# A two-layer mLSTM and RG-LRU trunk on one core: pair 7 of the FFN's input product in seven products, and half of its output weights' low halves by accumulating DMAs

## The chip, the core and the metric

The kernel runs on one core of a Trainium2 chip. A core has five engines with instruction queues of their own: TensorE (PE, with its weight loads as PEld) multiplies, VectorE (DVE) and ScalarE (ACT) work element by element, GpSimd (POOL) does a few small things and can issue DMAs, SyncE (SP) issues most DMAs. Each engine takes its instructions in the order in which they stand in its queue and waits on semaphores for the others. The metric is the time of one execution on the device, in microseconds (us); less is better.

## What is computed

One sequence of 256 tokens with 2048 features goes through two layers. Layer 0 has a chunkwise mLSTM mixer, layer 1 an RG-LRU mixer; each is followed by a SwiGLU feed-forward network (FFN), all in float32:

```python
D_MODEL, SEQ, D_FF = 2048, 256, 5632

def swiglu(x, w_in, w_out):
    g, u = jnp.split(x @ w_in, 2, axis=-1)
    return (jax.nn.silu(g) * u) @ w_out

for layer in range(2):
    h = h + mixer(rms_norm(h, norm_mix[layer]), ...)
    h = h + swiglu(rms_norm(h, norm_ffn[layer]), ffn_w_in[layer], ffn_w_out[layer])
return rms_norm(h, norm_final)
```

The change lies in the FFN, which runs once in each layer.

## The kernel before

**Three matmuls for one product.** TensorE takes operands rounded to a shorter float32 form (`F32R`). Every operand is therefore split into a rounded high half and the rest as a low half (`split`: ACT rounds, DVE subtracts), and a product takes three matmuls: high by high, high by low, low by high (`product`, lines 819 to 821). Of each weight tile, 512 KB or 1 MB in float32, ACT makes `whi` and DVE makes `wlo`.

**The FFN's loop.** `ffn` walks over j = 0 to 10, each a block of 512 of the 5632 inner columns; one pass is called a turn here. In a turn `inner` multiplies the 256 tokens by the gate and the up block of the first weights. The 2048 input features are taken as eight pairs p = 0 to 7 of row tiles of 128. A pair is a two by two block product: two row tiles of the features by two token halves, against gate (B11, B21) and up (B12, B22) blocks. A *plain* pair takes eight products (24 matmuls of 512 columns); a pair in `SEVENS` takes seven (21 matmuls) by Strassen's scheme in Winograd's form: DVE first makes four sums T1 to T4 of the weight blocks (`sum`, lines 312, 315, 316), so there are seven weight tiles to split, three of raw blocks (`whix`, `wlox`, 128x1536) and four of sums (`whit`, `wlot`, two instructions of 128x1024 each). The features' side of the seven (`SEVEN`) is prepared once per layer by `NormPairs.pair`.

**The banks.** Seven PSUM banks hold the sums: Q5, P2, Q3 and P4, which a plain pair writes too, and P1, Q6 and P7, which only pairs in seven products write. Pair 7 is plain and is the last, so P1, Q6 and P7 are complete after pair 6; then ACT copies P1 to `ds` (line 853) and DVE forms d0 and d1 from Q6 and P7 (lines 854, 856). After pair 7 DVE adds Q5, P2, Q3 and P4 (lines 859 to 865), ACT applies silu, DVE multiplies (line 868): these are the 512 inner activations of 256 tokens in `ds`. In the next turn PE transposes them (`tv`), and ACT and DVE split them into `hh`. In turn 0 pairs 1 to 4 (`BOTH`) are plain too.

**The second layer of the FFN.** For each turn's `hh`, `outs` makes eight pieces: a quarter q of the 2048 output columns by a token half b, 12 matmuls each (`out`). They are put between the products of the next turn, one per pair, from pair 4 of one turn to pair 3 of the one after. Ahead of b = 0, the quarter's weights come in two loads of 512 KB by SP (`rawo`, i = 0 and 1), and each is split into `whio` and `wloo`. These tiles have one buffer for each i. The last pieces of a layer use other tiles.

**What sets the order.** The code is recorded with priorities, and a scheduler with its own estimates sets the order in each engine's queue; splits and combinations have a raised priority. `whi` and `wlo` of the first weights have three buffers each, in rotation over all weight tiles of the pairs; the raw tiles too.

Of the kernel before, what the change touches and what calls it, by code (L numbers as in the profile page):

```python
# [42 lines left out]
def kernel(  # L43
# [117 lines left out]
    mask = const.tile([P, P], F32, name="mask")  # L161
    nc.gpsimd.memset(mask, 0.0)
    nc.gpsimd.affine_select(
        out=mask, in_=mask, compare_op=ALU.is_ge, fill=BIG, base=0,
        pattern=[[1, P]], channel_multiplier=-1,
    )
# [631 lines left out]
    def ffn(layer, n, nxt):  # L798
# [86 lines left out]
        def outs(j, hi, lo):  # L885
# [7 lines left out]
            def load(q, last):  # L893
# [9 lines left out]
                for i in range(2):  # L903
                    raw, wh, wl = (
                        pool_of(f"{what}o").tile([P, 2, NB], dt, tag=f"{what}{i}", name=f"{what}o{j}{q}{i}")
                        for what, dt in (("raw", F32), ("whi", F32R), ("wlo", F32R))
                    )
                    nc.sync.dma_start(raw, wv[:, 2 * i:2 * i + 2, q * NB:(q + 1) * NB])
# [300 lines left out]
```

## Time and profile before

| | |
|---|---|
| Median of 3 runs | 2086.08 us (2085.92 to 2087.57) |
| The profiled execution | 2085.02 us, of which the instructions' span is 2083.2 us |
| PE busy | 2069.3 us, 99% of the span |
| DVE busy | 1742.1 us, 84% |
| ACT busy | 1343.0 us, 64% |
| POOL busy | 43.2 us, 2% |
| Granted TensorE clock, mean | 0.999 |
| HBM read | 401.84 MB, 194 GB/s over the span |
| The FFN of layer 0, of layer 1 | from about 398 us, and from about 1383 us |

An engine's busy time says how much of the span it had something to do, not that it set the pace. A wait counts where an engine that sets the pace stands still. Rows of groups give the line of the code, the engine, the operation, out<-in by tile names, and behind the bar the busy time, the mean duration in ns, and idle time with its releaser.

### The profile page before, as it was taken

To read this page: it belongs to the slowest core of one execution; us is meant where nothing else is said; L and a number is where in the kernel's file an instruction comes from. 1 tells how busy PE (TensorE), PEld (TensorE's weight loads), DVE (VectorE), ACT (ScalarE), POOL (GpSimd) and SP (SyncE) were. 2 spreads that over 40 slices of the span, in tenths; PEclk is the share of its full clock that TensorE was granted. 3 is DMA by queue.
4 is the path that set the end of the run, shared out by engine and by line. 5 is a ranking of instruction groups with operands and counts; after the bars stand their busy time and mean duration, and the time that the engine had idled before them with its cause. 6 is when DMAs were issued, how large, how long until landed. Compare 5 with 4: busy or idle time off the path is not lost.

```text
span 2083.2 us, 27536 instructions
## 1 busy us (share of the span) xinstructions
PE 2069.3 (99%) x10484; PEld 1752.6 (84%) x10484; DVE 1742.1 (84%) x1898; ACT 1343.0 (64%) x1627; POOL 43.2 (2%) x62
## 2 busy tenths in 40 slices
PE   9999999999999999999999999999999999999998
PEld 8988888887888888888889999888788888888886
DVE  6655556699999999999976787679999999999995
ACT  6344446566777676777764768556676776776774
POOL 0011110000000000000000000000000000000002
PEclk9999999999999999999999999999999999999999
DMA  7555656555665566565555665655556556566653
GB/s 229 171 162 177 178 181 222 190 173 200 206 215 198 192 216 208 200 216 192 185 179 161 192 187 189 219 207 181 201 204 222 195 186 208 201 211 212 202 188 135
DMA packets 211901, 405.75 MB, mean 195 GB/s; under 512 B 15080, under 2 KB 15800, under 8 KB 211640
## 3 DMA queue, kind: packets, MB, share of 16 engines
q1 hardware_dynamic: 211048, 402.92, 58.5%
q8 instruction: 82, 1.34, 0.3%
q10 hardware_dynamic: 720, 1.07, 0.1%
q14 instruction: 51, 0.42, 0.1%
HBM read 401.84 MB, written 2.10 MB: 194 GB/s over the span
## 4 chain that ended last, share of the span: by engine, by line
PE 93%; DVE 4%; ACT 1%; issue 1%; DMA 1%; POOL 0%; ACTq 0%; POOLq 0%; SPq 0%; DVEq 0%
PE P L820 7%; PE P L821 7%; PE out L819 7%; PE P L819 7%; PE out L821 7%; PE out L820 7%; PE Q L820 6%; PE Q L821 6%; PE Q L819 6%; PE po L330 3%; PE po L328 3%; PE po L329 3%; PE o L330 1%; PE v L328 1%; PE rec L347 1%; PE v L329 1%
## 5 line engine op out<-in xcount | busy, mean ns | idle before, releaser
L244 DVE TENSOR_TENSOR wlo<-raw,whi 128x1024 fp32r<-128x1024 f32 (+1 forms) x226 | 273.4, 1213 | 171.4 <-ACT whi L243 170.8
L243 ACT CAST whi<-raw 128x1024 fp32r<-128x1024 f32 (+1 forms) x226 | 234.7, 1043 | 196.7 <-PE po L330 43.3
L268 ACT CAST whit<-sum 128x1024 fp32r<-128x1024 f32 x248 | 255.1, 1052 | 145.0 <-DVE sum L316 79.4
L269 DVE TENSOR_TENSOR wlot<-sum,whit 128x1024 fp32r<-128x1024 f32 x248 | 297.2, 1220 | 20.0 <-ACT whit L268 20.0
L819 PE MATMUL out<-whio,hh 128*128 128x512 f32 x704 | 275.1, 391 | 0.1
L820 PE MATMUL out<-wloo,hh 128*128 128x512 f32 x704 | 274.1, 389 | 0.0
L821 PE MATMUL out<-whio,hh 128*128 128x512 f32 x704 | 273.9, 389 | 0.0
L269 DVE TENSOR_TENSOR wlox<-raw,whix 128x1536 fp32r<-128x1536 f32 x124 | 217.3, 1753 | 12.1 <-ACT whix L268 12.1
L268 ACT CAST whio<-rawo 128x1024 fp32r<-128x1024 f32 (+1 forms) x166 | 183.5, 1106 | 64.3 <-PE out L821 54.7
L269 DVE TENSOR_TENSOR wloo<-rawo,whio 128x1024 fp32r<-128x1024 f32 (+1 forms) x166 | 209.8, 1283 | 3.0 <-ACT whio L268 2.5
L268 ACT CAST whix<-raw 128x1536 fp32r<-128x1536 f32 x124 | 184.0, 1484 | 38.5 <-PE P L821 16.1
L938 ACT COPY h<-out 128x512 f32<-128x512 f32 x154 | 89.9, 584 | 126.1 <-PE out L821 125.8
L312 DVE TENSOR_TENSOR sum<-raw 128x1024 f32<-128x1024 f32 x124 | 151.5, 1222 | 7.0 <-DMA raw<-in_ffn_w_in_dram 2.6
L819 PEld LDWEIGHTS out<-whio,hh 128*128 128x128 f32 x704 | 132.1, 188 | 29.6 <-ACT out L927 1.8
L821 PEld LDWEIGHTS out<-whio,hh 128*128 128x128 f32 x704 | 132.1, 188 | 27.8
L820 PEld LDWEIGHTS out<-wloo,hh 128*128 128x128 f32 x704 | 132.2, 188 | 27.2
L269 DVE TENSOR_TENSOR wlo<-raw,whi 128x2048 fp32r<-128x2048 f32 x52 | 117.5, 2288 | 28.8 <-ACT whi L268 28.8
L268 ACT CAST whi<-raw 128x2048 fp32r<-128x2048 f32 x52 | 97.4, 1911 | 24.0 <-DMA raw<-in_ffn_w_in_dram 17.7
L819 PE MATMUL P<-whix,p_f 128*128 128x512 f32 x248 | 97.6, 399 | 1.8 <-ACT whix L268 1.8
L819 PE MATMUL Q<-whit,p_f 128*128 128x512 f32 x248 | 97.2, 392 | 0.8 <-ACT whit L268 0.8
L927 ACT COPY out<-h 128x512 f32<-128x512 f32 x156 | 91.9, 589 | 8.3 <-DVE h L936 6.7
L820 PE MATMUL P<-wlox,p_f 128*128 128x512 f32 x248 | 97.1, 391 | 0.2
(293 smaller groups left out, 5023.5 us busy)
## 6 DMA issues: line engine op xcount, KB each, us to landing
raw<-in_ffn_w_in_dram SPq DMA_DIRECT2D x352, 512.0 KB, 4.5
rawo<-in_ffn_w_out_dram SPq DMA_DIRECT2D x176, 512.0 KB, 4.9
raw<-in_m_w_in_dram SPq DMA_DIRECT2D x94, 512.0 KB, 3.7
raw<-in_r_w_in_dram SPq DMA_DIRECT2D x64, 512.0 KB, 4.4
raw<-in_m_w_out_dram SPq DMA_DIRECT2D x32, 512.0 KB, 3.8
raw<-in_r_w_out_dram SPq DMA_DIRECT2D x32, 512.0 KB, 4.3
...
```

Source lines behind the costliest of these rows:

```text
L243: nc.scalar.copy(hi[:, i:i + step, 0:ncols], r)
L244: nc.vector.tensor_tensor(lo[:, i:i + step, 0:ncols], r, hi[:, i:i + step, 0:ncols].bitcast(F32), op=ALU.subtract)
L268: nc.scalar.copy(hi, src)
L269: nc.vector.tensor_tensor(lo, src, hi.bitcast(F32), op=ALU.subtract)
L312: nc.vector.tensor_tensor(t[:, 0:2, :], raw[:, 1:3, :], raw[:, 3:4, :].broadcast_to([P, 2, NB]), op=ALU.add)
L328: nc.tensor.matmul(o, lhsT=ah[:, bs], rhs=hi, start=(k == 0), stop=False)
L329: nc.tensor.matmul(o, lhsT=ah[:, bs], rhs=lo, start=False, stop=False)
L819: nc.tensor.matmul(o, lhsT=a[0], rhs=b[0], start=start, stop=False, **kw)
L820: nc.tensor.matmul(o, lhsT=a[0], rhs=b[1], start=False, stop=False, **kw)
L821: nc.tensor.matmul(o, lhsT=a[1], rhs=b[0], start=False, stop=stop, **kw)
L927: nc.scalar.copy(o, hs)
L938: nc.scalar.copy(hs, o)
```

## The change

Pair 7 joins `SEVENS`. It is then the last pair in seven products as well as the last pair, so all seven banks are complete only in it; its products are emitted in the order `LAST` (P1, Q6, P7 first), each with its stop flag. On the features' side, pair 7 is prepared as the other pairs in seven are.

In the second layer of the FFN, the tile i = 1 of each quarter no longer gets its low half from DVE. ACT writes the negative of the rounded rows to `wloo` (the copy with scale -1), and a DMA that POOL issues reads the same weights from memory once more and adds them in place, which leaves the low half; a second copy of ACT makes `whio`. For odd q this tile has a buffer of its own (the place `wloo1`). To make room, the mask, the scratch tiles (`junk`) and two tiles of the norms move to other pools.

```diff
@@ constants @@
-SEVENS = (1, 2, 3, 4, 5, 6)
+SEVENS = (1, 2, 3, 4, 5, 6, 7)
...
+LAST = tuple(sorted(PRODUCTS, key=lambda c: ("P1", "Q6", "P7", "Q5", "P2", "Q3", "P4").index(c[0])))
@@ places of the FFN @@
-        "raw1", "raw2", "sum0", "rawo", "whio", "wloo", "wlo1", "whi1", "wlo2", "whi2", "raw0", "whi0", "wlo0",
+        "raw1", "raw2", "sum0", "rawo", "whio", "wloo", "wlo1", "whi1", "wlo2", "whi2", "raw0", "whi0", "wlo0", "wloo1",
@@ class NormPairs: the scratch of the squares (in Norm: pool x) @@
+        def junk(self):
+            place, tag = ("c", "junk") if "c" in pools else ("rawo", "raw1")
+            return pool_of(place).tile([P, NB], F32, tag=tag, name="junk")
@@ inner @@
                     work = [
-                        (c, seven[a], ops[b], p == SEVENS[-1] and c in ("P7", "P1", "Q6")) for c, a, b in PRODUCTS
+                        (c, seven[a], ops[b], p == SEVENS[-1])
+                        for c, a, b in (LAST if p == SEVENS[-1] else PRODUCTS)
                     ]
@@ outs, load @@
                 for i in range(2):
+                    spare = "1" if i and q % 2 else ""
                     raw, wh, wl = (
-                        pool_of(f"{what}o").tile([P, 2, NB], dt, tag=f"{what}{i}", name=f"{what}o{j}{q}{i}")
-                        for what, dt in (("raw", F32), ("whi", F32R), ("wlo", F32R))
+                        pool_of(f"{what}o{at}").tile([P, 2, NB], dt, tag=f"{what}{i}", name=f"{what}o{j}{q}{i}")
+                        for what, dt, at in (("raw", F32, ""), ("whi", F32R, ""), ("wlo", F32R, spare))
                     )
-                    nc.sync.dma_start(raw, wv[:, 2 * i:2 * i + 2, q * NB:(q + 1) * NB])
+                    src = wv[:, 2 * i:2 * i + 2, q * NB:(q + 1) * NB]
+                    nc.sync.dma_start(raw, src)
                     with tc.high_priority(offset=AHEAD):
-                        split(wh, wl, raw)
+                        if i:
+                            nc.scalar.activation(wl, raw, AF.Copy, scale=-1.0)
+                            nc.gpsimd.dma_start(wl, src, accum_op=ALU.add)
+                            nc.scalar.copy(wh, raw)
+                        else:
+                            split(wh, wl, raw)
```

Left out are the mask's move to the mixer's pool and `junk`, `dg` and `rbc` going to the pool x or the mixer's. Line numbers below belong to the kernel that is shown: with the change, 268 and 269 become 264 and 265, 312 to 316 become 308 to 312, 819 to 821 become 828 to 830, 853 to 868 become 863 to 878.

Where it moves instructions, layer 0, the end of turn 4: in the names, `P1_4` or `ds4` is turn 4's, `wlox4_7` belongs to turn 4, pair 7, `wlo5_0` to the next turn's pair 0, `wloo320` to the piece weights of turn 3's `hh`, quarter 2, tile i = 0; the number at the end counts buffers. DVE, before:

```order
L269 TENSOR_TENSOR wlot4_6_5767<-sum4_6_5758,whit4_6_5766 128x1024
L269 TENSOR_TENSOR wlo4_7_5827<-raw4_7_5823,whi4_7_5826 128x2048
L269 TENSOR_TENSOR wlo5_0_5883<-raw5_0_5879,whi5_0_5882 128x2048
L854 TENSOR_TENSOR ds4_5386<-Q6_4_5512,ds4_5386 128x512
L312 TENSOR_TENSOR sum5_1_5958<-raw5_1_5955 128x1024
L856 TENSOR_TENSOR ds4_5386<-ds4_5386,P7_4_5508 128x512
L315 TENSOR_TENSOR sum5_1_5958<-sum5_1_5958,raw5_1_5955 128x512
L859 TENSOR_TENSOR ds4_5386<-Q5_4_5394,ds4_5386 128x2x512
L862 TENSOR_TENSOR ds4_5386<-P2_4_5401,ds4_5386 128x512
```

and with the change:

```order
L265 TENSOR_TENSOR wlox4_7_5876<-raw4_7_5868,whix4_7_5875 128x1536
L265 TENSOR_TENSOR wlot4_6_5814<-sum4_6_5805,whit4_6_5813 128x1024
L308 TENSOR_TENSOR sum4_7_5871<-raw4_7_5868 128x1024
L311 TENSOR_TENSOR sum4_7_5871<-sum4_7_5871,raw4_7_5868 128x512
L312 TENSOR_TENSOR sum4_7_5871<-sum4_7_5871,raw4_7_5868 128x512
L265 TENSOR_TENSOR wlot4_7_5880<-sum4_7_5871,whit4_7_5879 128x1024 x2
L308 TENSOR_TENSOR sum5_1_6014<-raw5_1_6011 128x1024
L864 TENSOR_TENSOR ds4_5430<-Q6_4_5557,ds4_5430 128x512
L265 TENSOR_TENSOR wlo5_0_5938<-raw5_0_5934,whi5_0_5937 128x2048
L866 TENSOR_TENSOR ds4_5430<-ds4_5430,P7_4_5553 128x512
L872 TENSOR_TENSOR ds4_5430<-P2_4_5445,ds4_5430 128x512
L869 TENSOR_TENSOR ds4_5430<-Q5_4_5438,ds4_5430 128x2x512
```

Pair 7's one subtraction became seven instructions ahead of the combinations, and P2 is combined ahead of Q5. ACT at the same place, before:

```order
L268 CAST whix4_6_5762<-raw4_6_5755 128x1536
L927 COPY out301_5731<-h_73 128x512
L268 CAST whit4_6_5766<-sum4_6_5758 128x1024
L268 CAST whio310_5788<-rawo310_5787 128x1024
L938 COPY h_73<-out301_5731 128x512
L268 CAST whio311_5794<-rawo311_5793 128x1024
L268 CAST whit4_6_5766<-sum4_6_5758 128x1024
L927 COPY out310_5799<-h_73 128x512
L853 COPY ds4_5386<-P1_4_5480 128x512
L268 CAST whi4_7_5826<-raw4_7_5823 128x2048
```

and with the change (925 is the negated copy, 927 the cast beside it, 946 and 957 the copies that were 927 and 938):

```order
L927 CAST whio311_5841<-rawo311_5840 128x1024
L946 COPY out310_5847<-h_73 128x512
L264 CAST whix4_7_5875<-raw4_7_5868 128x1536
L264 CAST whit4_6_5813<-sum4_6_5805 128x1024
L925 ACTIVATE wloo321_5970<-rawo321_5968 128x1024
L264 CAST whit4_7_5879<-sum4_7_5871 128x1024
L957 COPY h_73<-out310_5847 128x512
L264 CAST whit4_7_5879<-sum4_7_5871 128x1024
L946 COPY out311_5897<-h_73 128x512
L863 COPY ds4_5430<-P1_4_5525 128x512
```

The negated copy of the next quarter's tile stands ahead of pair 7's two `whit` casts. PE, from pair 7's start, before:

```order
L819 MATMUL Q5_4_5394<-whi4_7_5826,p7_f0_3764 128x512
L820 MATMUL Q5_4_5394<-wlo4_7_5827,p7_f0_3764 128x512
L821 MATMUL Q5_4_5394<-whi4_7_5826,p7_f0_3764 128x512
L819 MATMUL Q5_4_5394<-whi4_7_5826,p7_f0_3764 128x512
L820 MATMUL Q5_4_5394<-wlo4_7_5827,p7_f0_3764 128x512
L821 MATMUL Q5_4_5394<-whi4_7_5826,p7_f0_3764 128x512
```

and with the change:

```order
L828 MATMUL P1_4_5525<-whix4_7_5875,p7_f0_3770 128x512
L829 MATMUL P1_4_5525<-wlox4_7_5876,p7_f0_3770 128x512
L830 MATMUL P1_4_5525<-whix4_7_5875,p7_f0_3770 128x512
L828 MATMUL P7_4_5553<-whit4_7_5879,p7_f0_3770 128x512
L828 MATMUL Q6_4_5557<-whit4_7_5879,p7_f0_3770 128x512
L829 MATMUL P7_4_5553<-wlot4_7_5880,p7_f0_3770 128x512
L830 MATMUL P7_4_5553<-whit4_7_5879,p7_f0_3770 128x512
L828 MATMUL Q5_4_5438<-whit4_7_5879,p7_f0_3770 128x512
L829 MATMUL Q5_4_5438<-wlot4_7_5880,p7_f0_3770 128x512
L829 MATMUL Q6_4_5557<-wlot4_7_5880,p7_f0_3770 128x512
L830 MATMUL Q6_4_5557<-whit4_7_5879,p7_f0_3770 128x512
L830 MATMUL Q5_4_5438<-whit4_7_5879,p7_f0_3770 128x512
```

P1, P7, Q6 and Q5 come first, then the piece `out311`, then P2, Q3 and P4, nine matmuls; the next turn then starts with five matmuls of P2 where it started with Q5.

More of the change, by code (lines that the diff above doesn't have):

```diff
@@ L160 @@
     nc.vector.memset(mhalf, -0.5)
[L161 to L166, printed above, removed]
     par_src = [
@@ L378, in __init__ @@
             self.ss = small.tile([P, NT, 4], F32, tag="ss", name=f"ss_{name}")
+        def junk(self):
+            return pool_of("x").tile([P, NB], F32, tag="junk", name="junk")
         def stats(self, q, blocks=range(NT)):
@@ L383, in stats @@
                 if junk is None:
-                    junk = small.tile([P, NB], F32, tag="junk", name="junk", bufs=1)
+                    junk = self.junk()
                 nc.scalar.activation(
@@ L442, in finish @@
             if self.bcast:
-                dg = small.tile([P, NT, P], F32, tag="dg", name=f"dg_{self.name}", bufs=1)
+                dg = pool_of("x").tile([P, NT, P], F32, tag="dg", name=f"dg_{self.name}")
                 for b in range(NT):
@@ L447, in finish @@
                 nc.tensor.matmul(pb[:, 0:T], lhsT=ones, rhs=dg.rearrange("p b t -> p (b t)"), start=True, stop=True)
-                self.bc = small.tile([P, T], F32, tag="rbc", name=f"rbc_{self.name}")
+                self.bc = pool_of("x").tile([P, T], F32, tag="rbc", name=f"rbc_{self.name}")
                 nc.scalar.copy(self.bc, pb[:, 0:T])
@@ L456, in __init__, with junk @@
             self.more = {}
+        def junk(self):
+            place, tag = ("c", "junk") if "c" in pools else ("rawo", "raw1")
+            return pool_of(place).tile([P, NB], F32, tag=tag, name="junk")
         def pair(self, p):
@@ L574, in mlstm_mixer @@
             nc.gpsimd.tensor_copy(sel, ident[0:H, 0:H].unsqueeze(2).broadcast_to([H, H, P]))
+            mask = mx.tile([P, P], F32, name="mask", bufs=1)
+            nc.gpsimd.memset(mask, 0.0)
+            nc.gpsimd.affine_select(
+                out=mask, in_=mask, compare_op=ALU.is_ge, fill=BIG, base=0,
+                pattern=[[1, P]], channel_multiplier=-1,
+            )
             gw = mx.tile([P, NK, 2 * H], F32, name="gw", bufs=1)
@@ L728, in head_out @@
                     nc.vector.tensor_scalar_mul(hn[:, b, a, :], pv[:, 0:DV], den[:, 0:1])
-                    junk = small.tile([P, NB], F32, tag="junk", name="junk", bufs=1)
-                    nc.scalar.activation(junk[:, 0:DV], hn[:, b, a, :], AF.Square, accum_out=den[:, 1:2])
+                    junk = mx.tile([P, DV], F32, tag="junk", name="junk", bufs=1)
+                    nc.scalar.activation(junk, hn[:, b, a, :], AF.Square, accum_out=den[:, 1:2])
                     nc.vector.tensor_scalar(
@@ L1139, in mean @@
         def mean(self, q, b, src):
-            junk = small.tile([P, NB], F32, tag="junk", name="junk", bufs=1)
-            nc.scalar.activation(junk, src, AF.Square, scale=D ** -0.5, accum_out=self.ss[:, b, q:q + 1])
+            nc.scalar.activation(self.junk(), src, AF.Square, scale=D ** -0.5, accum_out=self.ss[:, b, q:q + 1])
         def scaled(self, q, b):
```

## The prediction

> **What bounds the kernel now.** I read the page's busy table first, then the windows by stage, then the timeline of single engines at the places where TensorE stops.
>
> ```profile
> PE 2069.3 (99%) x10484; PEld 1752.6 (84%) x10484; DVE 1742.1 (84%) x1898; ACT 1343.0 (64%) x1627; POOL 43.2 (2%) x62
> 418.00:505.00 87.00, 84.91 (x369) 67.48 (x368) 83.33 (x81) 52.88 (x56) 0.00 (x0) 1.00 0.54 183
> 505.00:600.00 95.00, 95.00 (x429) 78.85 (x428) 91.61 (x88) 68.08 (x77) 0.00 (x0) 1.00 0.59 202
> 669.10:731.20 62.10, 62.10 (x279) 51.51 (x278) 58.79 (x57) 43.95 (x50) 0.00 (x0) 1.00 0.60 203
> 1404.00:1491.00 87.00, 84.91 (x370) 67.29 (x369) 83.21 (x80) 53.22 (x56) 0.00 (x0) 1.00 0.54 184
> ```
>
> The window rows give length, then busy time of PE, PEld, DVE, ACT and POOL, the granted clock, DMA share and GB/s. 669.10:731.20 is one whole turn of the FFN's loop over j: PE has no gap, DVE works 58.79 of 62.10 us, so it is 3.3 us from being the bound. 418:505 and 1404:1491 are the end of turn 0 and all of turn 1 in the two layers: there DVE is busy 83.3 of 87 us and PE loses time. PE's own step and such a loss:
>
> ```profile
> 641.02 0.39 PE L820 MATMUL P<-wlot,p_f 128*128 128x512 f32 x1
> 641.25 0.39 PE L821 MATMUL P<-whit,p_f 128*128 128x512 f32 x1
> 641.48 0.39 PE L819 MATMUL out<-whio,hh 128*128 128x512 f32 x1
> ...
> 474.55 0.39 PE L821 MATMUL out<-whio,hh 128*128 128x512 f32 x1
> 475.83 0.73 PE L819 MATMUL P<-whix,p_f 128*128 128x512 f32 x2 [0.89 <-ACT whix L268]
> ```
>
> A duration says 0.39, but matmuls overlap; from start to start it is 0.226 us, the price I use. Between 474.55 and 475.83 stand 1.28 us instead of 0.226.
>
> **Part 1, fewer products.** Pair 7 takes 7x3 instead of 8x3 matmuls, in 22 turns: 66 x 0.226 = 14.9 us less, 0.68 a turn, all on the bound.
>
> **Part 2, what DVE gains and loses.** By form, mean ns behind the comma:
>
> ```profile
> L269 DVE TENSOR_TENSOR wlot<-sum,whit 128x1024 fp32r<-128x1024 f32 x248 | 297.2, 1220 | 20.0 <-ACT whit L268 20.0
> L269 DVE TENSOR_TENSOR wlox<-raw,whix 128x1536 fp32r<-128x1536 f32 x124 | 217.3, 1753 | 12.1 <-ACT whix L268 12.1
> L269 DVE TENSOR_TENSOR wloo<-rawo,whio 128x1024 fp32r<-128x1024 f32 x156 | 186.9, 1219 | 0.5
> L268 ACT CAST whio<-rawo 128x1024 fp32r<-128x1024 f32 x156 | 164.5, 1054 | 59.4 <-PE out L821 52.0 <-DMA rawo<-in_ffn_w_out_dram 6.3
> L312 DVE TENSOR_TENSOR sum<-raw 128x1024 f32<-128x1024 f32 x124 | 151.5, 1222 | 7.0 <-DMA raw<-in_ffn_w_in_dram 2.6 <-issue 1.2 <-DVE ds L854 1.0
> L269 DVE TENSOR_TENSOR wlo<-raw,whi 128x2048 fp32r<-128x2048 f32 x52 | 117.5, 2288 | 28.8 <-ACT whi L268 28.8
> L315 DVE TENSOR_TENSOR sum<-sum,raw 128x512 f32<-128x512 f32 x124 | 85.3, 688 | 1.6
> L316 DVE TENSOR_TENSOR sum<-sum,raw 128x512 f32<-128x512 f32 x124 | 85.2, 687 | 1.5
> ```
>
> Pair 7 costs DVE 1.22+0.69+0.69+1.75+2x1.22 = 6.79 where it cost 2.29: +4.50 busy, and +4.1 start to start, since each of the five further instructions overlaps its neighbour by 0.08. The accumulating DMAs take off half of the 156 wloo: 78 x 1.14, four a full turn, 4.5 start to start. A full turn of DVE thus becomes 0.4 shorter, 58.4 of a PE turn of 61.4: still not the bound on average. ACT gets 4 x 1.05 for the negated copies (the form nearest: the whio cast) and 1.48+2x1.05-1.91 = 1.7 for pair 7, so some 49.5 of 61.4; its queue order matters below, its sum doesn't.
>
> **Part 3, where the two don't cancel: turns 0 and 1.** Few second-layer loads fall there: of the wloo whose removal counts, two lie in 418:505, while both turns' pair 7 do. DVE's work in that stretch becomes 83.3 + 2x4.1 - 2x1.14 + 0.8 (pair 7 of the input now has four small subtractions and a wider split ahead of it) = 90 us, in a stretch of 87 in which DVE had 3.7 us idle. If none of it is put off, the stretch needs 90 to 94; if all can be put off into turn 2 (DVE has 95-91.6 = 3.4 us to spare in 505:600), it needs 87-1.4. Following DVE's new order row by row with these prices, I get the first transposes of turn 2 about 3 us later than before, since wlox and wlot of turn 0's pair 7 come to PE late and wlo of turn 2's pair 0 now stands ahead of wlot of turn 1's. I take +3.0 a layer, with ends -1.4 and +5.5; the two layers have the same rows, so +6.0.
>
> **Part 4, the end of each later turn.** Before, P1, P7 and Q6 were complete at pair 6, and their combination ran beside pair 7's products. Now they complete in pair 7. DVE's rows there:
>
> ```profile
> 733.63 4.49 DVE L269 TENSOR_TENSOR wlo<-raw,whi 128x2048 fp32r<-128x2048 f32 x2 [1.19 <-ACT whi L268]
> 738.04 0.69 DVE L854 TENSOR_TENSOR ds<-Q,ds 128x512 f32<-128x512 f32 x1
> 738.65 1.22 DVE L312 TENSOR_TENSOR sum<-raw 128x1024 f32<-128x1024 f32 x1
> 739.78 0.68 DVE L856 TENSOR_TENSOR ds<-ds,P 128x512 f32<-128x512 f32 x1
> ...
> 743.31 1.75 DVE L269 TENSOR_TENSOR wlox<-raw,whix 128x1536 fp32r<-128x1536 f32 x1
> 744.98 0.68 DVE L864 TENSOR_TENSOR ds<-Q,ds 128x512 f32<-128x512 f32 x1
> 474.30 1.48 ACT L268 CAST whix<-raw 128x1536 fp32r<-128x1536 f32 x1 [2.98 <-PE P L821]
> ```
>
> Start to start: 2.2 for a plain wlo, 0.61 for 512 columns, 1.13 for 1024, 1.67 for wlox. The last row is ACT's cast, released by a PE product: with three whi buffers, pair 7's whix waits for pair 5's last matmul. From there (time 0, pair 6 begins on PE) ACT has whix at 1.8; DVE then does wlox 1.67, one wlot 1.13, three sums 2.6, two wlot 2.27, the next turn's first sum 1.13, Q6's combination 0.61, the next wlo 2.2, P7's 0.61 and P2's 0.68: 12.9, so P2's bank is free at 14.7 plus about 0.2 of waits. PE wants that bank after 21+12+21+12 = 66 matmuls: 14.93. The two meet. On the way Q6 wants the second whit and wlot at 8.4 and 9.5, and by the chain they come 0.1 and 0.15 late. I take 0.2 a turn (from 0 to 0.7) for the nine later turns of each layer: 18 x 0.2 = 3.6 us.
>
> **Part 5, the accumulating DMA.** No row shows one. The nearest is the plain load of the same 512 KB:
>
> ```profile
> L908 SPq DMA_DIRECT2D rawo<-in_ffn_w_out_dram x77: 367/368/415, 409.0 to 1041.8; - x77
> ...
> DMA to landing us min/median/max: 3.6/4.9/6.8
> ```
>
> (In the answer on the tile rawo.) The negated copy stands on ACT well ahead of the use: by the prices above, on the scale of part 4, it ends at 4.9 and the third k of the piece that reads the tile comes at 20, so some 15 us lie between. At 4.9, or at twice that, the DMA is covered; each us beyond 15 would be up to a us for each such tile, four a turn. I take nothing, with ends 0 and, were it 16, up to 4 a turn. [...] POOL's queue has nothing else to do in the FFN. The mask, the scratch tiles and the norm's tiles move to other pools at no cost: they are first-use work on POOL and ACT that stands before 410 us or between the layers, and no PE row waits there for them.
>
> **The sum.** Turns 2 to 10 of both layers: -18 x 0.68 = -12.2; turns 0 and 1: +6.0; turn ends: +3.6; together -2.6. The profiled execution took 2085.02 (span 2083.2 and 1.8 around it), so 2082.4; the median of the runs lies 1.06 higher, hence 2083.5. A difference of 0.2%, 4.2 us, is about what can be told from none.
>
> **Rivals.** *More of the gain stays* (faster). If DVE's backlog of turn 1 is put off into turn 2 (+1 instead of +3 a layer) and the turn ends wait for nothing, it is 2086.1-12.2+2 = 2076; with everything hidden 2071. For it: DVE's 3.3 us of slack a turn, and ACT's wide gaps; against: in 418:505 DVE had hardly a gap. *ACT blocked by a landing* (slower). ACT runs in order, and at the turn's end the negated copy, which waits for rawo, stands ahead of pair 7's whit. That load is issued at about 0 on the scale of part 4, and whit is free to start at 5.9 with a copy of 1.05 before it: a landing up to 4.9 us costs nothing, one of 6.8, the slowest above, 1.9 us of PE. From a mean wait of 0.58 a turn on (part 4's 0.2 included) the kernel is over 0.2% slower: 18 x (0.68-0.58) = 1.8 of gain against 6.0; with 1.0 a turn 2098. What could lengthen the landings is the added traffic, four 512 KB a turn on a share of 0.60; against it, this load is the first of its burst. [...] *The accumulation itself late*: at 16 us in place of 4.9, slower too, up to 18 x 4 = 72 us, about 2155; nothing but the missing row speaks for it.
>
> **Chances.** The forecast's band (2082 to 2090) 0.42, more of the gain 0.36, a blocked ACT 0.18, a late accumulation 0.04. So faster 0.36, same 0.42, slower 0.22. Range 2073 to 2096: it leaves out the full gain (0.06) and a wait of about 0.9 a turn or more (0.1).
>
> **What would show it.** Right: a full turn of 61.4 to 61.8 between two P1 copies; DVE near 58.4 in it; turns 0 and 1 with more PE waits on whix, whit or wlox than before; few waits of ACT for rawo. Wrong: turns of 62 or more with ACT's L925 waiting for a DMA, or PE waiting on wloo; or no added wait in 418:505.

## The result and the profile after

The changed kernel took 2121.52 us (median of 5 runs, 2119.67 to 2123.92) against 2086.01 us of the kernel before, run beside it (5 runs, 2085.37 to 2087.57): a ratio of 1.017, with a 95% interval of 1.0155 to 1.0185. It is 35.5 us slower; 2083.5 had been forecast, with 2096 as the upper end. Its profiled execution has a span of 2118.2 us, 35.0 more than before.

From the page of the changed kernel: the engines, POOL's DMA queue, and the landings of the three kinds of load.

```profile
PE 2074.1 (98%) x10418; PEld 1737.8 (82%) x10418; DVE 1756.5 (83%) x1936; ACT 1438.4 (68%) x1749; POOL 135.4 (6%) x140
...
q0 software_dynamic: 21216, 40.90, 12.3%
...
L925 ACT ACTIVATE wloo<-rawo 128x1024 fp32r<-128x1024 f32 x78 | 82.8, 1062 | 144.3 <-DMA rawo<-in_ffn_w_out_dram 144.3
...
raw<-in_ffn_w_in_dram SPq DMA_DIRECT2D x352, 512.0 KB, 6.5
rawo<-in_ffn_w_out_dram SPq DMA_DIRECT2D x176, 512.0 KB, 5.7
...
wloo<-in_ffn_w_out_dram POOLq DMA_DIRECT2D x78, 512.0 KB, 6.3
```

PE does the forecast's 66 matmuls fewer and still has 4.8 us more busy time. The accumulating DMAs land in 6.3 us. ACT stands still 144 us at the negated copies (L925), which wait for `rawo`: before, it waited 6.3 us for that tile.

To see where the 35 us lie, I divide the layer at the start of each turn's first Q5 product, in both traces: turns 0, 1 and 4 of layer 0, before, and then with the change (length, then busy PE, PEld, DVE, ACT, POOL, clock, DMA share, GB/s).

```profile
397.80:441.09 43.29, 43.29 (x195) 35.80 (x196) 36.70 (x35) 25.97 (x27) 0.72 (x1) 1.00 0.65 224
441.09:496.99 55.90, 53.81 (x231) 41.73 (x230) 54.47 (x54) 34.52 (x37) 0.00 (x0) 1.00 0.53 179
621.54:683.64 62.10, 62.10 (x280) 51.50 (x278) 58.80 (x57) 43.95 (x50) 0.00 (x0) 1.00 0.60 203
```

```profile
398.53:454.02 55.49, 48.64 (x203) 38.16 (x204) 43.21 (x45) 30.80 (x32) 3.31 (x3) 0.97 0.67 204
454.02:513.67 59.65, 56.67 (x237) 42.73 (x238) 56.11 (x57) 38.15 (x42) 1.20 (x1) 1.00 0.60 185
634.78:697.76 62.98, 62.04 (x277) 50.74 (x275) 58.93 (x58) 48.53 (x56) 4.81 (x4) 1.00 0.80 235
```

Turn 0 is 12.2 us longer, turn 1 3.7, this full turn 0.9. Over everything: 0.7 ahead of the FFN, 24.7 in the two turns 0 (12.2 and 12.5), 7.7 in the two turns 1, 1.9 in the other 18. But these lengths mix lost time with moved work. With the change other products stand ahead of a turn's first Q5: turns 0 and 1 hold 203 and 237 matmuls instead of 195 and 231, although pair 7 takes three fewer in each. Some 20 matmuls, 4.5 us, are thus work of the later turns, and turns 2 and 3 are 1.9 and 1.5 us shorter for it (turns 4 to 9 of this layer are 0.4 to 1.4 longer).

So I also add up how long PE stands: what its steps from one matmul to the next have beyond 0.226 us, where a step is over 0.3 us. In the changed kernel PE stands 10.1 us longer than before in turn 0 of layer 0, 2.1 in turn 1 and 10.7 in turns 2 to 10; in layer 1 it is 10.4, 2.1 and 10.7. That makes 24.7 us in the turns 0 and 1, and 21.4 us, 1.2 a turn, in the other 18: the full turns lose as much as the start.

**Turn 0, seen from PE backwards.** Timelines of ACT, DVE and PE of the changed kernel (start, duration, and in brackets the idle time ahead with its releaser):

```profile
407.41 1.05 ACT L925 ACTIVATE wloo<-rawo 128x1024 fp32r<-128x1024 f32 x1
...
409.30 0.82 ACT L472 ACTIVATE c_f<-tr_f,cols 128x256 f32<-128x256 f32 x2
418.78 1.06 ACT L925 ACTIVATE wloo<-rawo 128x1024 fp32r<-128x1024 f32 x1 [8.66 <-DMA rawo<-in_ffn_w_out_dram]
419.75 0.93 ACT L264 CAST p_f<-c_f 128x896 fp32r<-128x896 f32 x1
```

```profile
420.71 1.09 DVE L265 TENSOR_TENSOR p_f<-c_f,p_f 128x896 fp32r<-128x896 f32 x1 [3.74 <-ACT p_f L264]
...
450.86 0.68 DVE L872 TENSOR_TENSOR ds<-P,ds 128x512 f32<-128x512 f32 x1
```

```profile
431.39 0.39 PE L830 MATMUL P<-whit,p_f 128*128 128x512 f32 x1
433.85 0.50 PE L828 MATMUL P<-whix,p_f 128*128 128x512 f32 x1 [2.07 <-ACT whix L264]
435.64 0.50 PE L829 MATMUL P<-wlox,p_f 128*128 128x512 f32 x1 [1.29 <-DVE wlox L265]
...
436.33 0.63 PE L828 MATMUL P<-whix,p_f 128*128 128x512 f32 x1
436.76 0.63 PE L829 MATMUL P<-wlox,p_f 128*128 128x512 f32 x1
...
451.60 0.50 PE L828 MATMUL P<-whi,p_f 128*128 128x512 f32 x1 [1.60 <-DVE ds L872]
```

The second negated copy of the layer stands in ACT's queue ahead of the split of pair 6's features; it waits 8.66 us for a load that was issued at 409.42, right behind four loads of the first weights, and took 9.3 us to land. (Before, such a load took up to 8.5 us here, and nothing on ACT waited for it. ACT stood at this place then too, 7.50 us for DVE's `c_f`, but the split of the features began at 415.96 instead of 419.75.) DVE then waits 3.74 us. From 434 on PE waits for pair 6's `whix` and `wlox`, and at 451.60 for the bank P2, which DVE frees late behind pair 7's new work.

**A full turn.** The same three engines at the end of turn 5:

```profile
748.24 1.06 ACT L925 ACTIVATE wloo<-rawo 128x1024 fp32r<-128x1024 f32 x1 [1.66 <-DMA rawo<-in_ffn_w_out_dram]
749.91 1.06 ACT L264 CAST whit<-sum 128x1024 fp32r<-128x1024 f32 x1 [0.61 <-DVE sum L308]
...
751.34 1.05 ACT L264 CAST whit<-sum 128x1024 fp32r<-128x1024 f32 x1
```

```profile
748.60 1.23 DVE L308 TENSOR_TENSOR sum<-raw 128x1024 f32<-128x1024 f32 x1
749.86 0.69 DVE L311 TENSOR_TENSOR sum<-sum,raw 128x512 f32<-128x512 f32 x1
750.58 0.69 DVE L312 TENSOR_TENSOR sum<-sum,raw 128x512 f32<-128x512 f32 x1
```

```profile
751.47 0.39 PE L828 MATMUL P<-whit,p_f 128*128 128x512 f32 x1
752.44 0.50 PE L828 MATMUL Q<-whit,p_f 128*128 128x512 f32 x1 [0.58 <-ACT whit L264]
```

ACT waits 1.66 us for the landing, as the rival had it; but the first whit then waits 0.61 us more for DVE's sum, and the second starts at 751.34, right after DVE's L312 ends at 751.27. PE loses 0.75 us at Q6's second whit, and 0.73 to 1.03 at this place in each of turns 3 to 9 of this layer (0.47 to 1.10 in layer 1). Which of the two is late, ACT's wait or DVE's row, the trace alone does not settle.

### The profile page after: what moved, and what is told of

Its sections match the earlier page's. It is cut to its first block, busy times and chain, and to the rows that moved or that the text cites. A ratio compares the mean times of both kernels' runs of the same rounds, so it can differ in the third digit from the quotient of the medians.

```text
span 2118.2 us, 27777 instructions
## 1 busy us (share of the span) xinstructions
PE 2074.1 (98%) x10418; PEld 1737.8 (82%) x10418; DVE 1756.5 (83%) x1936; ACT 1438.4 (68%) x1749; POOL 135.4 (6%) x140
## 4 chain that ended last, share of the span: by engine, by line
PE 80%; ACT 7%; DVE 6%; DMA 4%; issue 3%; POOL 0%; ACTq 0%; POOLq 0%; SPq 0%; DVEq 0%
PE out L828 6%; PE out L829 6%; PE out L830 6%; PE P L829 5%; PE P L830 5%; PE P L828 5%; PE Q L828 5%; PE Q L829 5%; PE Q L830 4%; DMA rawo<-in_ffn_w_out_dram 4%; PE po L324 3%; PE po L326 3%; PE po L325 3%; DVE wlox L265 2%; DVE wlot L265 1%
## 5 line engine op out<-in xcount | busy, mean ns | idle before, releaser
L264 ACT CAST whit<-sum 128x1024 fp32r<-128x1024 f32 x292 | 305.5, 1049 | 108.0 <-DVE sum L308 87.7
L265 DVE TENSOR_TENSOR wlot<-sum,whit 128x1024 fp32r<-128x1024 f32 x292 | 355.0, 1221 | 23.6 <-ACT whit L264 22.7
L265 DVE TENSOR_TENSOR wlox<-raw,whix 128x1536 fp32r<-128x1536 f32 x146 | 256.0, 1754 | 13.8 <-ACT whix L264 13.2
L264 ACT CAST whix<-raw 128x1536 fp32r<-128x1536 f32 x146 | 216.0, 1480 | 26.0 <-PE P L830 22.3
L308 DVE TENSOR_TENSOR sum<-raw 128x1024 f32<-128x1024 f32 x146 | 178.6, 1224 | 10.0 <-DMA raw<-in_ffn_w_in_dram 5.9
L925 ACT ACTIVATE wloo<-rawo 128x1024 fp32r<-128x1024 f32 x78 | 82.8, 1062 | 144.3 <-DMA rawo<-in_ffn_w_out_dram 144.3
L926 POOL DMA_DIRECT2D wloo<-in_ffn_w_out_dram x78 | 94.0, 1206 | 1229.3 <-ACT wloo L925 918.9
L828 PEld LDWEIGHTS out<-whio,hh 128*128 128x128 f32 x704 | 132.1, 188 | 29.7 <-ACT out L946 1.2
L828 PE MATMUL Q<-whit,p_f 128*128 128x512 f32 x292 | 117.1, 401 | 12.5 <-ACT whit L264 12.5
L828 PE MATMUL P<-whix,p_f 128*128 128x512 f32 x292 | 114.8, 399 | 9.0 <-ACT whix L264 9.0
L264 ACT CAST whio<-rawo 128x1024 fp32r<-128x1024 f32 (+1 forms) x88 | 101.0, 1147 | 33.1 <-PE out L830 23.9
L265 DVE TENSOR_TENSOR wloo<-rawo,whio 128x1024 fp32r<-128x1024 f32 (+1 forms) x88 | 117.9, 1339 | 5.6 <-ACT whio L264 5.5
L829 PE MATMUL P<-wlot,p_f 128*128 128x512 f32 x292 | 114.0, 390 | 1.7 <-DVE wlot L265 1.7
L830 PE MATMUL P<-whix,p_f 128*128 128x512 f32 x292 | 114.6, 393 | 0.0
```

Source lines behind the costliest of these rows:

```text
L264: nc.scalar.copy(hi, src)
L265: nc.vector.tensor_tensor(lo, src, hi.bitcast(F32), op=ALU.subtract)
L308: nc.vector.tensor_tensor(t[:, 0:2, :], raw[:, 1:3, :], raw[:, 3:4, :].broadcast_to([P, 2, NB]), op=ALU.add)
L828: nc.tensor.matmul(o, lhsT=a[0], rhs=b[0], start=start, stop=False, **kw)
L829: nc.tensor.matmul(o, lhsT=a[0], rhs=b[1], start=False, stop=False, **kw)
L830: nc.tensor.matmul(o, lhsT=a[1], rhs=b[0], start=False, stop=stop, **kw)
```

## The experiments

The theories: **A**, ACT blocked by landings at L925; **B**, DVE's backlog from pair 7's products, with the waits on ACT between its instructions; **C**, the traffic of POOL's queue. Each run stood beside runs of the kernel before, whose medians lay between 2085.16 and 2085.71. The table gives the ratio with its interval and, in us against the kernel before, the lengths of turn 0 and turn 1 (layer 0 / layer 1) and the sum of layer 0's turns 2 to 10. Where pair 7 changes, these lengths have the moved work in them, so the last column gives how much longer PE stands in turn 0, in turn 1 and in turns 2 to 10 of layer 0. The diffs are excerpts, against the changed kernel; moves of small tiles to other pools and of stop flags, which some runs need, are left out.

| run | us | ratio (95%) | turn 0 | turn 1 | turns 2-10 | PE stands, 0 / 1 / 2-10 |
|---|---|---|---|---|---|---|
| changed kernel | 2121.52 | 1.017 (1.0155-1.0185) | 12.2 / 12.5 | 3.7 / 3.9 | +1.2 | 10.1 / 2.1 / 10.7 |
| e1 POOL negates | 2152.27 | 1.0324 (1.0309-1.034) | 13.3 / 13.7 | 3.3 / 3.0 | +18.7 | 11.3 / 1.7 / 29.1 |
| e2 seven products alone | 2160.36 | 1.0361 (1.0345-1.0376) | 9.4 / 10.8 | 3.4 / 3.4 | +24.3 | 7.3 / 2.3 / 29.7 |
| e3 accumulation alone | 2098.53 | 1.0069 (1.0052-1.0085) | 3.8 / 7.1 | 0.3 / -0.1 | -0.5 | 3.7 / 0.4 / -0.3 |
| e4 no accumulating DMA | 2112.84 | 1.0136 (1.0121-1.0151) | 8.6 / 9.3 | 3.7 / 3.8 | +0.7 | 6.4 / 2.0 / 10.7 |
| f1 ACT's order set | 2119.85 | 1.0163 (1.0147-1.018) | 5.8 / 6.9 | 7.9 / 8.0 | +0.2 | 4.5 / 5.6 / 9.9 |
| f2 pair 5 plain in turn 0 | 2118.03 | 1.0153 (1.0138-1.0168) | 9.7 / 12.0 | 4.1 / 4.3 | +3.5 | 7.7 / 1.6 / 13.3 |
| f3 pair 7 plain in turn 0 | 2105.44 | 1.0093 (1.0078-1.0108) | 1.3 / 1.2 | 6.2 / 6.4 | +1.1 | 1.3 / 1.8 / 11.0 |
| f4 both of f1 and f3 | 2116.16 | 1.0144 (1.0128-1.0159) | 1.1 / 0.8 | 9.8 / 9.9 | +3.8 | 1.0 / 5.6 / 13.4 |
| g1 less for DVE | 2109.93 | 1.0119 (1.0102-1.0136) | 12.9 / 14.4 | 1.0 / 0.8 | -3.4 | 10.8 / -0.2 / 7.0 |
| g2 f3 and another LAST | 2128.87 | 1.0211 (1.0196-1.0227) | 0.6 / 1.0 | 6.8 / 6.9 | +14.1 | 0.5 / 2.3 / 25.1 |
| g3 e3 with turn 0's order | 2085.98 | 1.0004 (0.9995-1.0013) | 0.0 / -0.1 | 0.4 / 0.1 | -0.3 | 0.0 / 0.5 / -0.1 |
| h1 three quarters by DMA | 2150.32 | 1.0305 (1.0288-1.0321) | 2.2 / 4.7 | 5.5 / 5.6 | +22.8 | 2.0 / 0.7 / 33.1 |
| h2 h3 with less for DVE | 2092.8 | 1.0037 (1.0023-1.0051) | 0.4 / 1.5 | 3.5 / 3.4 | -4.8 | 0.4 / -0.5 / 5.5 |
| h3 f3 with turn 0's order | 2103.4 | 1.0083 (1.0068-1.0098) | 1.2 / 1.2 | 5.7 / 6.3 | -1.4 | 1.1 / 1.2 / 8.8 |
| i1 seven in every second turn | 2088.99 | 1.0015 (1.0006-1.0024) | 1.1 / 0.8 | 0.2 / 0.7 | -1.2 | 1.1 / 0.1 / 1.4 |
| i2 seven in two of three | 2088.48 | 1.0017 (1.0008-1.0026) | 0.7 / 1.5 | 0.2 / 0.6 | -1.0 | 0.6 / 0.1 / 2.9 |

**e1, POOL makes the negated copy.**

```diff
-                            nc.scalar.activation(wl, raw, AF.Copy, scale=-1.0)
+                            nc.gpsimd.tensor_scalar_mul(wl, raw, -1.0)
```

> The negated copy (L925) is taken from ACT and done by POOL, which has nothing else to do in the FFN; all else is as in the changed kernel. Theory A (ACT blocked by a landing: in the changed kernel L925 waits 76 times, 144 us in all, for rawo, with casts that TensorE needs behind it): ACT's waits for rawo fall below 20 us, the 12.2 us that turn 0 of each layer lost shrink to 5 or less, full turns come to 61.4 to 61.8 us, and the kernel takes 2075 to 2090 us. Theory B (DVE's backlog of pair 7's seven products in turns 0 and 1): ACT's waits go, but turn 0 still loses 8 us or more a layer, 2095 to 2110. Either would be hidden if POOL's copies slowed DVE: then DVE's busy time rises well above 1756 us.

From its page, then one form of DVE between 640 and 1000 us in this run and in the changed kernel:

```profile
L925 POOL TENSOR_SCALAR wloo<-rawo 128x1024 fp32r<-128x1024 f32 x78 | 277.1, 3552 | 959.7 <-DMA rawo<-in_ffn_w_out_dram 937.5
```

```profile
L265 DVE TENSOR_TENSOR wlox<-raw,whix 128x1536 fp32r<-128x1536 f32 x40 | 75.5, 1886 | 3.6 <-ACT whix L264 3.6
```

```profile
L265 DVE TENSOR_TENSOR wlox<-raw,whix 128x1536 fp32r<-128x1536 f32 x41 | 71.9, 1754 | 4.3 <-ACT whix L264 4.3
```

ACT is free of L925, and the kernel is 31 us slower than the changed one. The copy takes 3.55 us instead of 1.06, DVE's `wlox` subtractions are 8% longer (1886 ns instead of 1754) and its sums of 1024 columns 11% (1354 ns instead of 1224), while `wlot` stays (1229 and 1221): DVE's busy time rises by 51 us. The run does not judge A, as its expectation allowed; that it loses 31 us with less room for DVE fits B (in the full turns PE waits for whit and wlot, never for `wloo`).

**e2 and e3, each half of the change alone.** e2 splits all of the second layer as before; e3 leaves pair 7 plain.

```diff
 e2:  -                        if i: ...
      +                        split(wh, wl, raw)
 e3:  +SEVENS = (1, 2, 3, 4, 5, 6)
```

> Pair 7 in seven products with LAST's order, but every low half of the second layer by DVE as in the kernel before; no negated copy, no accumulating DMA. Theory A: ACT does not wait for rawo; DVE's turn is 58.8 + 4.1 = 62.9 us, over TensorE's 61.4, so full turns take 62.9 (18 x 0.8 = +14.6 against 2086), turns 0 and 1 add some 5 us a layer: about 2110. Theory B: turns 0 and 1 still add 12 to 16 us a layer, 2125 to 2132.

> SEVENS as before (pairs 1 to 6, pair 7 plain), but half of the second layer's low halves by the negated copy and the accumulating DMA. Theory A: ACT is blocked in turn 0 as in the changed kernel, so turn 0 loses 4 to 10 us a layer with no added work for DVE, and a full turn 0 to 1 us: 2094 to 2120. Theory B: DVE has less to do everywhere, so nothing is lost: 2078 to 2088.

Turns 0, 1 and 4 of e2, and of e3 turns 0 and 4 with ACT's wait over the whole run:

```profile
398.07:450.78 52.71, 48.67 (x204) 38.20 (x204) 45.76 (x48) 30.00 (x31) 0.73 (x1) 0.97 0.57 195
450.78:510.07 59.29, 56.35 (x237) 42.13 (x235) 55.96 (x55) 35.45 (x39) 0.00 (x0) 1.00 0.52 177
640.36:705.53 65.17, 63.84 (x276) 49.79 (x276) 63.13 (x62) 45.18 (x52) 0.00 (x0) 1.00 0.59 194
```

```profile
398.05:445.10 47.05, 43.85 (x195) 35.72 (x195) 35.36 (x34) 27.72 (x29) 3.31 (x3) 1.00 0.73 229
625.52:687.62 62.10, 62.10 (x280) 51.52 (x278) 55.08 (x53) 47.94 (x55) 4.82 (x4) 1.00 0.83 242
```

```profile
ACT wloo L925 <- DMA rawo<-in_ffn_w_out_dram: 122.1, 58, 10.2
```

The seven products alone cost 75 us, the accumulation alone 13, both together 35: the accumulation is what keeps DVE from 63.1 us a turn. e2 is slower than both its expectations: DVE's 63.1 us of work take 65.2 us of turn, 2 more than the 62.9 of A's sum, so DVE does not do its work without gaps. In e3 ACT waits 122 us at L925 and PE not at all in a full turn: 62.10 us, to the hundredth as before. Its whole loss is turn 0, where DVE has less to do than before and ACT waits 9 us. So both A and B cost time in turn 0, and in e3's full turns A costs nothing.

**e4, the accumulating DMA left out.**

```diff
-                            nc.gpsimd.dma_start(wl, src, accum_op=ALU.add)
```

> The accumulating DMA itself is left out (the low half of these tiles is then the negated rounded rows, without the rows added); the negated copy stays in its place. Theory A, with the wait set by ACT's own order: the load of rawo is issued at the end of the previous cast L927, and L925 stands 3 to 5 us behind, so at the old landing of 4.9 us it still waits about 1 us each, and turn 0, where other loads stand ahead of rawo, still waits over 5 us at once: 2103 to 2114. Theory C (the traffic of the second queue lengthens the landings and is the cause): landings of rawo fall back to 4.9 us, ACT's waits to under a third of 144 us, 2080 to 2096.

It gains 8.7 us, 6.7 of it in the two turns 0. ACT still waits 133.9 us at L925, and `rawo` lands in 5.6 us instead of 5.7: C in the form that was expected falls. What is shorter without the accumulating DMA is ACT's wait in turn 0, 6.20 us instead of 8.66, and the median landing of the first weights, 4.9 us instead of 6.5 (but it is 4.6 in e3, with the same traffic, so the traffic alone does not set it).

**f1, ACT's order set** (`after` issues the copy behind named instructions):

```diff
+                            held_by = ([mark["silu"]] if q == 3 or j == 0 and q == 1
+                                       else [mark["whit"]] if q == 2 or j == 0 else [])
+                            with after(*held_by):
+                                nc.scalar.activation(wl, raw, AF.Copy, scale=-1.0)
```

> The changed kernel with nothing left out; only ACT's order is set: the negated copy L925 of the third quarter of the second layer is issued after pair 7's second whit, that of the fourth quarter after the second silu (L876), and the two of turn 0 after that turn's last whit and last silu. Theory A (ACT blocked by a landing sets both the steady loss and part of turn 0's): full turns fall from some 62.8 to 61.4 to 61.8 us (18 x -1.0 = -18 or, since turns 2 and 3 had gained some of it back already, -11), and turn 0 loses 9 instead of 12.2 us: 2095 to 2108. Theory B (DVE's backlog alone): no change, 2116 to 2122.

ACT's wait over the run; PE's wait for whit between 574 and 1010 us in the changed kernel, then in f1; PE's wait for the accumulated `wloo` in f1; and turns 0 and 1:

```profile
ACT wloo L929 <- DMA rawo<-in_ffn_w_out_dram: 70.9, 49, 3.7
```

```profile
PE Q L828 <- ACT whit L264: 4.9, 7, 0.9
```

```profile
PE Q L830 <- ACT whit L264: 4.6, 7, 0.9
```

```profile
L831 PE MATMUL out<-wloo,hh 128*128 128x512 f32 x704 | 275.2, 391 | 6.9 <-DMA wloo<-in_ffn_w_out_dram 6.9
```

```profile
398.70:447.74 49.04, 45.50 (x199) 36.38 (x200) 42.16 (x45) 30.52 (x32) 2.11 (x2) 1.00 0.62 205
447.74:511.55 63.81, 58.35 (x240) 44.18 (x240) 60.66 (x60) 37.68 (x40) 2.40 (x2) 0.97 0.66 193
```

ACT's wait halves, and the time stays (2119.85). In the full turns no negated copy stands ahead of pair 7's whit any more, and PE waits for it as long as before (4.6 us against 4.9): A is refuted there. Turn 0 loses 5.8 us instead of 12.2, more than A promised (9). Turn 1 gives 4 of them back, but for a new reason: the later copies now come so late that PE waits for the accumulating DMA itself, once in each layer (6.9 us in the row, nothing in the changed kernel), and the mean clock of layer 0's turn 1 is 0.97 instead of 1.00. So f1's unchanged time is no proof against A in turns 0 and 1.

**f2, f3, f4: less of the seven products in turn 0.** f2 takes pair 5 plain there, f3 pair 7, f4 is f3 with f1's order.

```diff
 f2:  -BOTH = (1, 2, 3, 4)
      +BOTH = (1, 2, 3, 4, 5)
 f3:  +BOTH = (1, 2, 3, 4, 7)
      -                if p == SEVENS[-1]:
      +                if p == (SEVENS[-1] if j else 6):
```

> The changed kernel, but in turn 0 pair 5 is taken in eight plain products too (BOTH with 5), which takes 4.5 us from DVE there and adds 3 matmuls (0.7 us) to TensorE. Theory B (turn 0 is bound by DVE's backlog behind pair 7's seven products): turn 0 loses 6 to 8 instead of 12.2 us, 2109 to 2114. Theory A alone: turn 0 waits as long as before, 2119 to 2123.

> The changed kernel, but pair 7 is plain in turn 0 (as in the kernel before) and in seven products from turn 1 on; the accumulating DMAs and ACT's order stay. If pair 7's products in turn 0 cost what the run with the seven products alone showed (9.4 and 10.8 us) and the accumulation alone 3.8 and 7.1, turn 0 now loses 3 to 7 us a layer, turn 1 some 1 to 3.7, the rest as in the changed kernel: 2098 to 2110. If turn 0's loss is ACT's blocked 8.66 us and nothing else: 2115 to 2122.

> Both edits of the other runs together: pair 7 plain in turn 0, and ACT's order set for the negated copies. If the two causes add up, turn 0 loses 0 to 2 us a layer, turn 1 1 to 3, and the 18 full turns give 0.3 to 0.68 us each: 2076 to 2090, the first version not slower than the kernel before. If a third cause stands behind the full turns: 2095 or more.

Turns 0 and 1 of f3:

```profile
397.71:442.31 44.60, 43.59 (x194) 35.71 (x195) 36.72 (x39) 27.29 (x30) 2.11 (x2) 1.00 0.66 215
442.31:504.42 62.11, 59.13 (x250) 45.02 (x250) 59.47 (x60) 40.65 (x44) 2.40 (x2) 1.00 0.66 206
```

f3 brings turn 0 to 1.3 us and the kernel to 2105.44: 16 us of the 35 come from pair 7 in turn 0. Its turn 1 is 6.2 us longer only because it holds 250 matmuls instead of 231; PE stands 1.8 us longer in it. The same 4.5 us of DVE's work taken away at pair 5 (f2) bring 3.5 us in all, less than its expectation. So it is hardly DVE's sum over turn 0. What stands at its end is left: pair 7's seven instructions and the next turn's pair 1 ahead of the combinations that free P2 and Q5; no run moves these alone. f4 was worse than f3 by 11 us, where the sum of both causes had it faster: with f1's order for the later copies PE again waits 3.5 us in each turn 1 for the accumulated `wloo`.

**g1, less for DVE.** The low half that DVE still makes (i = 0) is left out.

```diff
-                            split(wh, wl, raw)
+                            nc.scalar.copy(wh, raw)
...
+                for k in range(2):
+                    tiles[k][1] = tiles[2 + k][1]
```

> The changed kernel, but the subtraction that DVE still does for the second layer (the low half of the first half of each quarter, 4 a full turn, 4.5 us) is left out: those products read the accumulated low half of the other half in its place. Copies, loads and accumulating DMAs stay. Theory B (DVE, run in its order with waits on ACT between, is what paces turns 1 to 10; it works 58.9 of 63 us and idles 4 in waits on ACT's casts): the stall of 0.7 to 1.0 us a turn before Q6's second whit goes, full turns take 61.4 to 61.8 us, turn 1 loses 0 to 1 instead of 3.7; turn 0, where few of these subtractions stand, still loses 10 to 12: 2094 to 2104. Theory A (landings block ACT): ACT waits for rawo as before, 2113 to 2122.

A full turn (turn 6), and ACT's wait over the run:

```profile
759.66:821.13 61.47, 61.47 (x276) 50.95 (x275) 55.62 (x54) 49.80 (x56) 4.82 (x4) 1.00 0.83 239
```

```profile
ACT wloo L925 <- DMA rawo<-in_ffn_w_out_dram: 62.6, 44, 9.8
```

Here are the forecast's 61.4 us, with PE busy throughout: every turn from 4 to 9 of layer 0 gains some 0.63 us. Turn 1 falls to 1.0, turn 0 stays. ACT's waits fall too, so this run alone would not tell A from B; f1 (no copy ahead of the whit, nothing gained in the full turns) and e3 (122 us of waits, nothing lost in them) do. The time, 2109.93, missed the expected 2094 to 2104 by turn 2, where PE stands 7.4 us longer (7.2 in layer 1): pair 7's whit is cast there behind a negated copy that waits 3.7 us for `rawo`. Turn 3 is 3.3 us shorter because it holds less work.

**g2 and g3.** g2 is f3 with P2 and Q3 earlier in `LAST`; g3 is e3 with only turn 0's two copies held back.

```diff
 g2:  -("P1", "Q6", "P7", "Q5", "P2", "Q3", "P4")
      +("P1", "P2", "Q3", "P7", "Q6", "Q5", "P4")
 g3:  +                            held_by = ([mark["silu"]] if j == 0 and q == 1
      +                                       else [mark["whit"]] if j == 0 and q == 0 else [])
```

> Pair 7 plain in turn 0 (2105.4 us when tried alone), and LAST's order changed so that P2 and Q3, which need only whix, stand ahead of the products on whit. If the stall at Q6's second whit is only a matter of a late cast, it is covered by 6 matmuls (1.36 us): full turns 61.4 to 61.8 us, 2088 to 2097. If DVE paces the turn, the stall moves to the next turn's first banks and the time stays: 2102 to 2109.

> The accumulating DMAs alone (pair 7 plain in all turns, 2098.5 us when tried), with the two negated copies of turn 0 issued after that turn's last whit and last silu on ACT. If those two waits of ACT for rawo are all that the accumulation costs: turn 0 loses 0 to 1 us instead of 3.8 and 7.1, 2085 to 2089. If traffic or the first load's place costs something: 2092 to 2099.

Turns 0 and 4 of g3:

```profile
397.94:441.26 43.32, 43.32 (x194) 35.80 (x195) 35.25 (x34) 26.92 (x28) 2.12 (x2) 1.00 0.66 210
621.88:683.97 62.09, 62.09 (x280) 51.50 (x278) 54.81 (x53) 47.27 (x54) 4.81 (x4) 1.00 0.80 233
```

g3 is the cleanest answer: with two copies of ACT moved, the accumulation costs nothing that can be told (1.0004), traffic and all. Where pair 7 is plain, A is the whole of e3's loss. g2 was slower than both its expectations (2128.87): covering one late cast moved the queues of the whole turn, and between 574 and 1010 us PE waits 4.9 us for ACT's copies into `out`, where the changed kernel has no such wait.

**h1, h2, h3.** All have pair 7 plain in turn 0 and g3's order; h1 has three of four row blocks by accumulating DMA, h2 g1's omission.

```diff
 h1:  -                for i in range(2):
      +                for i, (k0, n) in enumerate(((0, 1), (1, 3))):
```

> Three edits with nothing left out: pair 7 plain in turn 0; the two negated copies of turn 0 behind that turn's last whit and last silu on ACT; and three quarters of the second layer's low halves by accumulating DMA instead of half (a tile of one row block that DVE still subtracts, and one of three), which takes 2.3 us a turn from DVE (58.9 to 56.6 of 61.4, with 4 us of waits on ACT still inside) and gives ACT 2 us. Theory B (DVE with its waits paces the full turns): turn 0 loses 0 to 1 us, turn 1 0 to 4, full turns take 61.4 to 61.9 us: 2074 to 2088, at best the first version faster than the kernel before. If the added 20 MB of traffic or ACT's longer copies take its place as a bound: 2090 to 2110.

> Pair 7 plain in turn 0, the two negated copies of turn 0 behind that turn's last whit and silu, and the subtractions that DVE still does for the second layer left out (those products read the accumulated low half of the other half). If DVE's backlog in turn 0 and its pace in the later turns are all that cost time, turn 0 loses 0 to 1 us a layer, turn 1 0 to 1, and each full turn gains 0.63: 2073 to 2080. If turn 1 or 2 still lose 4 us a layer: 2081 to 2088. If something else remains: over 2090.

> Pair 7 plain in turn 0 and the two negated copies of turn 0 behind that turn's last whit and silu; the later turns as in the changed kernel. Pair 7 plain alone gave 2105.4 us, with turn 0 at 1.3, turn 1 at 6.2. Theory B: only turn 0's rest of some 1 us a layer can go, 2102 to 2106.

Turn 4 of h1; of h2 turn 5 and ACT in turn 2:

```profile
632.21:697.60 65.39, 63.49 (x276) 50.19 (x275) 56.52 (x58) 50.56 (x55) 5.11 (x4) 1.00 0.86 241
```

```profile
687.87:749.29 61.42, 61.42 (x277) 50.94 (x275) 55.59 (x54) 49.83 (x56) 4.81 (x4) 1.00 0.84 240
```

```profile
552.09 1.06 ACT L932 ACTIVATE wloo<-rawo 128x1024 fp32r<-128x1024 f32 x1 [3.46 <-DMA rawo<-in_ffn_w_out_dram]
553.06 1.03 ACT L264 CAST whit<-sum 128x1024 fp32r<-128x1024 f32 x1
```

h3 came as expected. h2 has full turns of 61.42, exactly 0.68 less than before, and came to 2092.8 rather than 2073 to 2080. Turn 1 is 3.5 us longer, but that is moved work (PE stands 0.5 less in it); what still loses is turn 2, where PE stands 5.9 us longer, and 8.5 in layer 1. There it is the rival as the prediction drew it: pair 7's whit behind a landing 3.46 us late. h1 missed by far. DVE has 56.5 us of work a turn, as expected, and the turn takes 65.4: copies of 1.49 us now stand on ACT between the casts for which DVE waits (91.3 us in all for whit, 22.7 in the changed kernel), and at the end of turn 5 pair 7's first whit stands behind one that has waited 2.30 us for its load. So DVE's sum alone does not pace a turn; the chain between DVE and ACT does, and work taken from the one and given to the other can lengthen it. How much of h1 is the longer copies and how much the landings stays open.

**i1 and i2, seven products in some turns only**, the other turns' pair 7 plain:

```diff
+TURNS = (3, 5, 7, 9)          # i2: (2, 3, 5, 6, 8, 9)
...
+        ... or p == 7 and j not in TURNS
```

> Nothing is left out. Pair 7 in seven products only in turns 3, 5, 7 and 9 of each layer, plain in the others; accumulating DMAs throughout, with the two negated copies of turn 0 behind that turn's last whit and last silu. If DVE with its waits paces a full turn (58.9 + 4 = 62.9 us with seven products, some 54.9 + 4 with plain ones, against TensorE's 61.4 and 62.1), a plain turn takes up what a seven turn leaves over, and 8 turns give up to 0.68 us each: 2078 to 2083 against 2085.5. If each such turn stalls by itself, whatever stands next to it: 2085 to 2092.

> As the run beside it, with pair 7 in seven products in turns 2, 3, 5, 6, 8 and 9. If a plain turn also takes up what two seven turns leave over (2 x 1.5 us against some 3): 12 x 0.68 = 8 us, 2077 to 2081. If DVE's backlog of two such turns in a row is too much: 2083 to 2095.

Neither gains (1.0015 and 1.0017). In i1 a plain turn and the seven turn behind it (turns 4 and 5) take 124.09 us together, against 124.19 before: 0.1 of the 0.68 arrives. PE stands 0.4 us longer than before in a seven turn and 0.1 in a plain one, where it is 1.2 a turn in the changed kernel, so a plain neighbour takes up most of the stall, not all of it; and turns 0 and 1 lose 1.3 and 1.5 us in the two layers. No version here beats the kernel before.

## Why the prediction was wrong

The sum was -2.6; the span grew by 35.0. Two steps failed, and about equally. In the prediction's terms PE was to stand 4.4 us a layer longer in turns 0 and 1 (+3.0, and the 1.4 of the fewer products with it), 8.7 in all; it stands 24.7 longer, 16 more. At the ends of the other 18 turns it was to stand 3.6 us; it stands 21.4, 18 more. The rest, some 4 us, is the start of the FFN (0.7) and pauses too short for this count.

- *Part 1, fewer products*: right. Where nothing else waits, a turn is 0.63 to 0.68 us shorter (g1, h2).
- *Part 2, DVE's and ACT's sums*: right in size, 58.9 and 48.5 us against 58.4 and 49.5 (ACT's terms as written add up to 49.8). The step from there was wrong: "still not the bound on average". 58.9 in a turn of 63 leaves 4 us, and 3.6 of them DVE spends waiting for ACT. The 3.3 us of slack in the kernel before were the same kind of gaps (3.1 of waits for ACT), not room.
- *Part 3, turns 0 and 1*: the first step that failed. +3.0 a layer was taken and +5.5 allowed, which is 4.4 and 6.9 of standing; measured 12.2 and 12.5. It summed DVE's work in 418 to 505 us, a stretch that starts after the worst wait (ACT, 410 to 418.8), and took a queue's work for its length. Pair 7's seven products alone make PE stand 9.6 and 10.9 us longer in these turns (e2), and ACT's wait for a landing, which the part put at nothing without a word, 4.1 and 6.7 when alone (e3). The two overlap. Some 1.6 us of each turn 0 is the half pace told of below, which was no term either.
- *Part 4, the end of a turn*: right place, wrong size, and the second step that failed. Q6's second whit was to come 0.1 us late and comes 0.73 to 1.03 late; with the slower steps behind such a wait (0.34 us at 752.44), and in some turns one of the transposes for `ds`, it is 1.2 a turn, where 0.2 was taken and 0 to 0.7 allowed. The chain begins later than priced: in turn 5 PE starts pair 6 at 743.31, and ACT, at copies until 744.2, ends whix at 745.62, 2.3 us on instead of 1.8. The second whit ends 9.1 us on, and Q6 wants it at 8.4.
- *Part 5, the accumulating DMA*: right. It lands in 6.3 us, and the cover between the copy's end and PE's first use is 12.9 to 15.9 us in the full turns (some 15 forecast). g3 shows it at no cost. What came with it, the copy on ACT, is where it cost; and where ACT's order delays that copy (f1, f4), PE does wait for the accumulation.
- *The rivals*: "ACT blocked by a landing" was given the right mechanism and the wrong place: at the turn's end it decides nothing while DVE is as late (f1); in turn 0, and in turn 2 of g1 and h2, it costs microseconds. Its traffic does not lengthen the median landing of `rawo` (5.7 us, and 5.6 in e4 without it). "More of the gain stays" needs DVE's idle time to be usable; it was not. The sign of 35 us was thus carried by a row that was read as slack.
